# Meta tokens transposed first, one half tile normalised on ACT, and gate multiplications tied to adds in two blocks only: a decoder layer with PEER experts

## The chip, the cores and the metric

The kernel is one program on one core of a Trainium2 chip. The core has a matrix engine (PE, with its weight loads shown apart as PEld), a vector engine (DVE), an engine for activations and copies (ACT), a general engine (POOL) and a queue engine that only issues transfers (SP). Each runs its own list of instructions strictly in the listed order, and semaphores tie the lists together. The metric is the device time of one execution in microseconds (us), given as the median over runs.

## The reference

One post-norm layer over 256 tokens of width 2048, with 16 learned meta tokens put in front. All is float32.

```
h    = layer_norm(concat(meta, x))                     # 272 x 2048
proj = h @ w_in                                        # 2048 -> 8192
ya   = pool mixer (windows 2/4/8/16) -> pool_w -> pool_scale -> pool_proj
yb   = gated short convolution (width 3)              -> conv_proj
h    = layer_norm(ALPHA * h + (gate0*ya + gate1*yb) @ w_out)
# PEER: 8 heads, top 16 of 128 x 128 = 16384 single-neuron experts
q    = h @ w_q ; scores against keys_1, keys_2 ; top 16 of the sums
gate = softmax(top scores)
act  = gelu(h . expert_u[idx]) ; y = sum(gate * act * expert_v[idx])
out  = layer_norm(ALPHA * h + y)[:, 16:]
```

## The kernel before

**Precision.** Every matmul operand is split into a high part and a low part (`hi`, `lo`) of a fast float32 format, and three products are added. For weights, ACT casts the high part (`whi`, L95) and DVE or POOL subtracts it to get the low part (`wlo`, L74). Such a pair is 128 x 1024 and is called a half tile here; a 1 MB load (`raw`, L84, issued by SP, three buffers) holds two of them. `whi` and `wlo` have three buffers each, so DVE can be at most three half tiles ahead of PE.

**Start.** The meta tokens (`mt`, in a tile named `lng`) and the two token tiles `res[:, 0]` and `res[:, 1]` get their statistics on DVE. ACT normalises the meta tokens (L206), DVE both token tiles in halves of 1024 (L151). PE transposes them by pieces of 128 features into `acc` (L218, L219), each piece of tile 0 together with 16 meta columns, so that `ht` is 144 wide. ACT applies gain and shift (L222), DVE casts (L225) and subtracts (L74) into `h_hl`. The input projection (L102 to L104, L108, L109) needs all 272 columns of a piece.

**Experts.** All 16384 experts are computed densely for 224 tokens, as 128 groups of 128, with the routing gates spread into a table `G`; the last 32 tokens are done by gathers (`lone`, `urow`). An up tile (`up`, L627) multiplies by `expert_u`, giving `gl`; DVE adds its two halves (L113), ACT takes the gelu (L625). A block is four groups. For each block, `coef` (L644) multiplies `gl` by its gates (L648, DVE, four per block, called the gate multiplications), ACT casts the product to `c_hi` (L77) and DVE subtracts to `c_lo` (L74); `down` (L730) multiplies these by `expert_v` in two column halves, four half tiles each (L660), and DVE adds the results into `res` (L669).

**The order.** 44 up tiles run first (`LEAD`). Then each of 32 blocks does its two `down` halves, with two more up tiles ahead of each until all 128 are done; that is so through block 20, and blocks 21 to 31 have no up tiles. The table `G` lies in DRAM (`spill`); for a block, seven transfers of 64 KB bring it to one of two buffers (`fetch`, L742, issued by SP at L745, one block ahead in the program). A scheduler sets the order on each engine from the program's order, priorities and its own idea of when operands are there; `issue_after(x)` forces an instruction to stand behind `x`. In the kernel before every gate multiplication stands behind `last_on["dve"]`, the last weight subtraction or addition that the program had put on DVE by then.

Of the kernel before, what the change touches and what calls it, by code (L numbers as in the profile page):

```python
# [8 lines left out]
F32 = mybir.dt.float32  # L9
# [5 lines left out]
OP = mybir.AluOpType  # L15
# [3 lines left out]
P = 128  # L19
D = 2048  # L20
KD = D // P
T = 256
NT = T // P
META = 16
# [11 lines left out]
NB = 4  # L36
# [17 lines left out]
def block(ctx, tc, x, meta, w_in, small, pool_w, projs, w_out, wq, keys, eu, eur, ev,  # L54
          ln1_g, ln1_b, ln2_g, ln2_b, lin_g, lin_b, out):
    nc = tc.nc

    def pool(stack, name, bufs, side="left"):
        return stack.enter_context(tc.tile_pool(name=name, bufs=bufs, side=side, reuse_waits="tile"))
# [7 lines left out]
    def ps_mm():  # L67
        return mm.tile([P, 512], F32, name="mm")

    def ps_acc(t, c):  # L70
        return accp.tile([P, 512], F32, name=f"acc{t}{c}")

    def lo_part(lo, full, hi, eng=None):
        return (eng or nc.vector).tensor_tensor(lo, full, hi.bitcast(F32), op=OP.subtract)  # L74

    def split(hi, lo, full):
        nc.scalar.copy(hi, full)  # L77
        lo_part(lo, full, hi)
# [9 lines left out]
    last_on = {}  # L88
# [35 lines left out]
    ident = const.tile([P, P], F32, name="ident")  # L124
# [14 lines left out]
    def stats(st, src, c, n):  # L139
        nc.vector.bn_stats(out=st[:n, c, :], in_=src)  # L140

    def st_tile():
        return const.tile([P, 4, 6], F32, name="st", bufs=4)

    def mean_rstd(st, n):
        mv = const.tile([P, 2], F32, name="mv", bufs=4)
        nc.vector.bn_aggr(out=mv[:n], in_=st[:n])
        return mv, rstd_of(mv, n)

    def normalize(eng, dst, src, mv, r, n):  # L150
        eng.tensor_scalar(dst, src, mv[:n, 0:1], r[:n], op0=OP.subtract, op1=OP.mult)  # L151

    def shift_of(mv, r, n):
        shift = const.tile([P, 1], F32, name="shift", bufs=4)
        nc.vector.scalar_tensor_tensor(shift[:n], mv[:n, 0:1], -1.0, r[:n], op0=OP.mult, op1=OP.mult)
        return shift
# [13 lines left out]
    with ExitStack() as pa:  # L170
# [3 lines left out]
        a2 = pool(pa, "a2", 1)  # L174

        mt = lnp.tile([P, D], F32, name="lng")
# [9 lines left out]
        g_in = sm[:, 40:56]  # L186
        b_in = sm[:, 56:72]
# [6 lines left out]
        h_hl = hp.tile([P, KD, 2, TT], F32R, name="h_hl")  # L194
        nc.scalar.activation(neghalf, neghalf, AF.Identity)
        srcs = ((mt[:META], META), (res[:, 0], P), (res[:, 1], P))
        for i, (src, n) in enumerate(srcs):
            st = st_tile()
            for c in range(4):
                stats(st, src[:, c * 512:(c + 1) * 512], c, n)  # L200
            mv, r = mean_rstd(st, n)
            shift = shift_of(mv, r, n)
            for c in range(2):
                part = src[:, c * 1024:(c + 1) * 1024]
                if i == 0:
                    nc.scalar.activation(part, part, AF.Identity, bias=shift[:n], scale=r[:n])  # L206
                else:
                    normalize(nc.vector, part, part, mv, r, n)
        for t in range(NT):
            t0, n = (META + P, P) if t else (0, META + P)  # L210
            for k0 in range(0, KD, 2):
                ps = ps_acc(k0 // 2 % 2, k0 // 4 % 2).rearrange("p (k t) -> p k t", k=2)
                ht = a2.tile([P, 2, META + P], F32, name="ht", bufs=4)
                for i in range(2):
                    k = k0 + i
                    ks = slice(k * P, (k + 1) * P)
                    if t == 0:
                        nc.tensor.transpose(ps[:, i, 0:META], mt[:META, ks], ident[:META, :META])  # L218
                    nc.tensor.transpose(ps[:, i, n - P:n], res[:, t, ks], ident)  # L219
                for i in range(2):  # L220
                    k = k0 + i
                    nc.scalar.activation(ht[:, i, :n], ps[:, i, :n], AF.Identity,  # L222
                                         bias=b_in[:, k:k + 1], scale=g_in[:, k:k + 1])
                h_hi = h_hl[:, k0:k0 + 2, 0, t0:t0 + n]
                nc.vector.tensor_copy(h_hi, ht[:, :, :n])  # L225
                lo_part(h_hl[:, k0:k0 + 2, 1, t0:t0 + n], ht[:, :, :n], h_hi)
# [109 lines left out]
        for m in range(KD):  # L336
# [10 lines left out]
            for (hi, lo), y in zip(halves(parts, praw), (ya, yb)):  # L347
                ps = ps_mm()
# [207 lines left out]
    with ExitStack() as pb:  # L556
# [87 lines left out]
        def coef(e):  # L644
            gl = gels.pop(e)
            glv = gl.rearrange("p (g t) -> p g t", t=TG)
            with tc.issue_after(last_on["dve"]):
                nc.vector.tensor_tensor(glv, glv, Gs[e // NB][:, :, e % NB], op=OP.mult)  # L648
            c_hi = coefp.tile([P, TD], F32R, name="c_hi")
            c_lo = coefp.tile([P, TD], F32R, name="c_lo")  # L650
            split(c_hi, c_lo, gl)
            coefs[e] = (c_hi, c_lo)
# [129 lines left out]
        for e0 in range(0, NKEY, NB):  # L782
            es = range(e0, e0 + NB)
            if e0 and es[-1] < NKEY - 1:
                fetch(e0 // NB + 1)
            for e in es:
                coef(e)
            for dh in range(2):
                for _ in range(NB // 2):
                    if n_up < NKEY:  # L790
                        tick(up(n_up, (None, nc.gpsimd)))
                        n_up += 1
                if dh == 0 or es[-1] < NKEY - 1:
                    tick(down(es, dh))
# [106 lines left out]
```

## Time and profile before

| what | us |
|---|---|
| median of 3 runs | 2117.13 (2116.28 to 2117.24) |
| profiled execution, whole | 2117.67 |
| span of its trace | 2115.9 |
| PE busy in the span | 2054.7 (97%) |
| DVE busy | 1525.5 (72%) |
| ACT busy | 1001.8 (47%) |

The span is what the instructions of the trace cover; 1.8 us of the execution lie around it. PE is the engine to look at: it is busy 97% of the span, so a change of time is a change of the few per cent in which it waits, or of the clock that it is granted. A row of the timeline gives start, duration, engine, line, operation, what is written and read, and how often it repeats in sequence (x4); in brackets stands how long the engine had been idle and what released it.

### The profile page before, as it was taken

The numbers are of one execution on the slowest core, as the hardware profiler recorded it, in microseconds if no ns is written. First come the engines' busy times: TensorE is split into PE (matmuls) and PEld (weight loads), VectorE is DVE, ScalarE is ACT, GpSimd is POOL, SyncE is SP. The second block draws the span as 40 slices with busy tenths as digits, with TensorE's granted clock in tenths as the row PEclk, the third lists the DMA queues.
The fourth block names the chain that finished last, engine by engine and source line by source line (L and its number), as shares of the span: only waits on it lengthen the run. The fifth ranks groups of instructions, "written<-read, shape, count | busy, mean of one in ns | idle before, by whom it ended". The sixth has DMA issues, their size and how long they took to land.

```text
span 2115.9 us, 29922 instructions
## 1 busy us (share of the span) xinstructions
PE 2054.7 (97%) x11558; PEld 1770.5 (84%) x11558; DVE 1525.5 (72%) x2340; ACT 1001.8 (47%) x1424; POOL 600.8 (28%) x294
## 2 busy tenths in 40 slices
PE   7999999999999699999999999999999999999997
PEld 6999888888888689998888888888888888877765
DVE  7766666666779878836767776776677677788878
ACT  5444544444443356554444444444444445444442
POOL 0000000000065588883332333232334232300001
PEclk9999999999999799999999999999999999999998
DMA  5555555566553357787878777878787877877654
GB/s 202 219 180 182 195 181 191 187 224 233 191 183 125 107 202 273 264 284 274 292 266 291 272 269 268 291 269 289 262 283 268 293 260 275 278 271 270 224 169 158
DMA packets 114334, 498.09 MB, mean 235 GB/s; under 512 B 11200, under 2 KB 38336, under 8 KB 73344
## 3 DMA queue, kind: packets, MB, share of 16 engines
q1 hardware_dynamic: 103584, 413.61, 56.8%
q0 software_dynamic: 10608, 82.58, 10.0%
q8 instruction: 90, 1.47, 0.3%
q14 instruction: 52, 0.43, 0.1%
HBM read 478.32 MB, written 16.78 MB: 234 GB/s over the span
## 4 chain that ended last, share of the span: by engine, by line
PE 90%; DVE 7%; issue 1%; DMA 1%; POOL 1%; ACT 1%; SPq 0%; POOLq 0%; ACTq 0%
PE mm L108 28%; PE acc L660 27%; PE mm L109 14%; PE mm L660 5%; PE mm L103 2%; PE mm L102 2%; PE mm L104 2%; PE acc L116 2%; PE acc L117 2%; PE acc L118 2%; PE mm L595 1%; POOL wlo L74 1%; DMA raw<-in_eu 0%; DVE res L669 0%; PE acc L219 0%
## 5 line engine op out<-in xcount | busy, mean ns | idle before, releaser
L95 ACT CAST whi<-raw 128x1024 fp32r<-128x1024 f32 x738 | 772.2, 1048 | 801.5 <-PE mm L108 256.4
L74 DVE TENSOR_TENSOR wlo<-raw,whi 128x1024 fp32r<-128x1024 f32 x546 | 684.7, 1257 | 471.8 <-ACT whi L95 468.3
L108 PE MATMUL mm<-x_hl,whi 128*128 128x448 f32 x2048 | 656.1, 379 | 18.6 <-DVE gl L113 16.8
L74 POOL TENSOR_TENSOR wlo<-raw,whi 128x1024 fp32r<-128x1024 f32 x192 | 490.9, 2563 | 587.1 <-ACT whi L95 282.9
L109 PE MATMUL mm<-x_hl,wlo 128*128 128x224 f32 x2048 | 544.4, 266 | 6.3 <-POOL wlo L74 6.1
L108 PEld LDWEIGHTS mm<-x_hl,whi 128*128 128x128 f32 x2048 | 387.7, 189 | 50.4 <-issue 17.2
L109 PEld LDWEIGHTS mm<-x_hl,wlo 128*128 128x128 f32 x2048 | 394.9, 193 | 10.3 <-POOL wlo L74 8.0
L660 PE MATMUL acc<-whi,c_lo 128*128 128x512 f32 (+1 forms) x832 | 260.7, 395 | 5.0 <-DVE c_lo L74 5.0
L660 PE MATMUL acc<-whi,c_hi 128*128 128x512 f32 (+1 forms) x832 | 260.8, 395 | 4.3 <-ACT c_hi L77 4.3
L660 PE MATMUL acc<-wlo,c_hi 128*128 128x512 f32 (+1 forms) x832 | 260.7, 395 | 0.0
L108 PE MATMUL mm<-h_hl,whi 128*128 128x512 f32 x640 | 225.0, 395 | 0.0
L136 POOL TENSOR_TENSOR rstd<-rstd,neghalf 128x1 f32<-128x1 f32 (+1 forms) x7 | 5.8, 821 | 713.8 <-DVE rstd L135 697.5
L660 PEld LDWEIGHTS acc<-whi,c_lo 128*128 128x128 f32 (+1 forms) x832 | 146.4, 176 | 52.7 <-DVE c_lo L74 6.4
L660 PEld LDWEIGHTS acc<-wlo,c_hi 128*128 128x128 f32 (+1 forms) x832 | 146.2, 176 | 46.1 <-issue 0.2
L660 PEld LDWEIGHTS acc<-whi,c_hi 128*128 128x128 f32 (+1 forms) x832 | 143.0, 176 | 47.5 <-ACT c_hi L77 4.8
L109 PE MATMUL mm<-h_hl,wlo 128*128 128x256 f32 x640 | 180.5, 282 | 0.0
L669 DVE SCALAR_TENSOR_TENSOR res<-res,acc 128x512 f32<-128x512 f32 x208 | 131.6, 679 | 22.6 <-PE acc L660 20.7
L108 PEld LDWEIGHTS mm<-h_hl,whi 128*128 128x128 f32 x640 | 120.4, 188 | 26.9
L625 ACT ACTIVATE gl<-gl 128x224 f32<-128x224 f32 x128 | 49.7, 389 | 168.8 <-DVE gl L113 168.8
L109 PEld LDWEIGHTS mm<-h_hl,wlo 128*128 128x128 f32 x640 | 121.3, 189 | 0.0
L103 PE MATMUL mm<-h_hl,whi 128*128 128x258 f32 (+3 forms) x384 | 110.4, 288 | 0.0
L102 PE MATMUL mm<-h_hl,whi 128*128 128x258 f32 (+3 forms) x384 | 109.3, 285 | 0.0
(189 smaller groups left out, 2586.4 us busy)
## 6 DMA issues: line engine op xcount, KB each, us to landing
raw<-in_eu SPq DMA_DIRECT2D x128, 1024.0 KB, 6.0
raw<-in_ev SPq DMA_DIRECT2D x128, 1024.0 KB, 5.6
raw<-in_w_in SPq DMA_DIRECT2D x64, 1024.0 KB, 4.9
raw<-in_projs SPq DMA_DIRECT2D x16, 1024.0 KB, 4.9
raw<-in_w_out SPq DMA_DIRECT2D x16, 1024.0 KB, 5.0
raw<-in_wq SPq DMA_DIRECT2D x16, 1024.0 KB, 4.8
spill<-wide POOLq DMA_DIRECT2D x7, 2048.0 KB, 7.9
G<-spill SPq DMA_DIRECT2D x212, 64.0 KB, 5.1
```

The source lines that it names most:

```text
L74: return (eng or nc.vector).tensor_tensor(lo, full, hi.bitcast(F32), op=OP.subtract)
L95: last_on["act"] = nc.scalar.copy(hi, raw[:, s]).ins
L102: nc.tensor.matmul(ps, whi, xhi, start=first, stop=False)
L103: nc.tensor.matmul(ps, whi, xlo, start=False, stop=False)
L104: nc.tensor.matmul(ps, wlo, xhi, start=False, stop=last)
L108: nc.tensor.matmul(ps[:, :2 * n].rearrange("p (s t) -> p s t", s=2), whi, xhl, start=first, stop=False)
L109: nc.tensor.matmul(ps[:, :n], wlo, xhl[:, 0], start=False, stop=last)
L116: nc.tensor.matmul(ps, xhi, whi, start=first, stop=False)
L117: nc.tensor.matmul(ps, xhi, wlo, start=False, stop=False)
L625: nc.scalar.activation(gl, gl, AF.Gelu)
L660: nc.tensor.matmul(ps[c][:n_t], c_[:, ts], v_[:, c * 512:(c + 1) * 512], start=e == first and n == 0, stop=e == last and n == 2)
L669: nc.vector.scalar_tensor_tensor(r, r, 1.0 if (t, dh, c) in added else ALPHA, ps[c][:n_t], op0=OP.mult, op1=OP.add)
```

## The change

Three edits. The 16 meta transposes are taken out of the loop and done ahead into one tile `mm`; DVE applies gain and shift to all of them in two instructions, casts and subtracts them, and the token pieces shrink from 144 to 128 columns. The second half of `res[:, 0]` is normalised on ACT and no longer on DVE. The gate multiplications of blocks 0 and 1 stay behind the last DVE operation, those of blocks 2 to 31 are no longer tied to anything.

```diff
@@ -202,20 +202,27 @@
             shift = shift_of(mv, r, n)
             for c in range(2):
                 part = src[:, c * 1024:(c + 1) * 1024]
-                if i == 0:
+                if i == 0 or (i == 1 and c == 1):
                     nc.scalar.activation(part, part, AF.Identity, bias=shift[:n], scale=r[:n])
                 else:
                     normalize(nc.vector, part, part, mv, r, n)
+        pm = ps_mm()[:, :KD * META].rearrange("p (k t) -> p k t", k=KD)
+        for k in range(KD):
+            nc.tensor.transpose(pm[:, k], mt[:META, k * P:(k + 1) * P], ident[:META, :META])
+        hm = a2.tile([P, KD, META], F32, name="hm", bufs=1)
+        shape = [P, KD, META]
+        nc.vector.tensor_tensor(hm, pm, g_in[:, :, None].to_broadcast(shape), op=OP.mult)
+        nc.vector.tensor_tensor(hm, hm, b_in[:, :, None].to_broadcast(shape), op=OP.add)
+        nc.vector.tensor_copy(h_hl[:, :, 0, :META], hm)
+        lo_part(h_hl[:, :, 1, :META], hm, h_hl[:, :, 0, :META])
         for t in range(NT):
-            t0, n = (META + P, P) if t else (0, META + P)
+            t0, n = META + t * P, P
             for k0 in range(0, KD, 2):
                 ps = ps_acc(k0 // 2 % 2, k0 // 4 % 2).rearrange("p (k t) -> p k t", k=2)
-                ht = a2.tile([P, 2, META + P], F32, name="ht", bufs=4)
+                ht = a2.tile([P, 2, P], F32, name="ht", bufs=4)
                 for i in range(2):
                     k = k0 + i
                     ks = slice(k * P, (k + 1) * P)
-                    if t == 0:
-                        nc.tensor.transpose(ps[:, i, 0:META], mt[:META, ks], ident[:META, :META])
                     nc.tensor.transpose(ps[:, i, n - P:n], res[:, t, ks], ident)
@@ -644,7 +651,7 @@
         def coef(e):
             gl = gels.pop(e)
             glv = gl.rearrange("p (g t) -> p g t", t=TG)
-            with tc.issue_after(last_on["dve"]):
+            with tc.issue_after(last_on["dve"]) if e < 2 * NB else ExitStack():
                 nc.vector.tensor_tensor(glv, glv, Gs[e // NB][:, :, e % NB], op=OP.mult)
```

The lines behind the first edit shift by 7, so the gate multiplication is L648 before and L655 in the changed kernel, and the transfers of `G` are L745 and L752.

On DVE, at the start of block 0's first `down` half, the list before goes straight from the addition that ends an up tile (`gl_9605`) through the subtractions of the next half tiles (`wlo`).

```order
L74 TENSOR_TENSOR wlo_9665<-raw_9662,whi_9664 128x1024
L113 TENSOR_TENSOR gl_9605<-gl_9605,mm_9564 128x224
L74 TENSOR_TENSOR wlo_9681<-raw_9662,whi_9680 128x1024
L74 TENSOR_TENSOR wlo_9699<-raw_9696,whi_9698 128x1024
L113 TENSOR_TENSOR gl_9654<-gl_9654,mm_9611 128x224
L74 TENSOR_TENSOR wlo_9718<-raw_9696,whi_9717 128x1024
```

In the changed kernel the same place holds the gate multiplications of block 2 (reading `G_9917`) and of block 3 (`G_10293`); the numbers of the tiles are six higher here, so `wlo_9687` is the former `wlo_9681`.

```order
L74 TENSOR_TENSOR wlo_9671<-raw_9668,whi_9670 128x1024
L113 TENSOR_TENSOR gl_9611<-gl_9611,mm_9570 128x224
L655 TENSOR_TENSOR gl_6957<-gl_6957,G_9917 128x224
L655 TENSOR_TENSOR gl_7028<-gl_7028,G_9917 128x224
L655 TENSOR_TENSOR gl_7088<-gl_7088,G_9917 128x224
L655 TENSOR_TENSOR gl_7167<-gl_7167,G_9917 128x224
L74 TENSOR_TENSOR wlo_9687<-raw_9668,whi_9686 128x1024
L74 TENSOR_TENSOR wlo_9705<-raw_9702,whi_9704 128x1024
L113 TENSOR_TENSOR gl_9660<-gl_9660,mm_9617 128x224
L655 TENSOR_TENSOR gl_7245<-gl_7245,G_10293 128x224
L74 TENSOR_TENSOR wlo_9724<-raw_9702,whi_9723 128x1024
```

Blocks 2 to 12 follow in this manner between block 0's first half and block 1's second half in the list; from there each gate multiplication stands behind its own up tile. Block 1, which is still tied, comes after block 5. The sets of blocks 3, 4 and 5 thus pass through one of the two `G` buffers one after the other, since block 1's set holds the other.

On SP, in the same stretch, the list before has between two sets of seven `G` transfers six 1 MB loads (`raw`).

```order
L84 DMA raw<-in_eu 128x2048
L84 DMA raw<-in_ev 128x2x1024 x2
L84 DMA raw<-in_eu 128x2048 x2
L84 DMA raw<-in_ev 128x2x1024
L745 DMA G<-spill_6430 128x128
L745 DMA G<-spill_6431 128x128
L84 DMA raw<-in_ev 128x2x1024
```

In the changed kernel one load stands between two sets, or inside one.

```order
L752 DMA G<-spill_6442 128x128
L84 DMA raw<-in_eu 128x2048
L752 DMA G<-spill_6436 128x128
L752 DMA G<-spill_6437 128x128
L752 DMA G<-spill_6438 128x128
L752 DMA G<-spill_6439 128x128
L752 DMA G<-spill_6440 128x128
L752 DMA G<-spill_6441 128x128
L752 DMA G<-spill_6442 128x128
L84 DMA raw<-in_eu 128x2048
```

In the changed list twelve sets of seven (blocks 3 to 14) stand among 14 loads; in the list before there are eight loads to each set.

On DVE at the change from block 28 to 29, near the end, the list before has the gate multiplications and the `c_lo` of the new block in one piece, behind the additions of the old one.

```order
L721 SCALAR_TENSOR_TENSOR res<-res,urow 32x2048
L74 TENSOR_TENSOR wlo<-raw,whi 128x1024 x2
L669 SCALAR_TENSOR_TENSOR res<-res,mm 128x512 x2
L74 TENSOR_TENSOR wlo<-raw,whi 128x1024
L669 SCALAR_TENSOR_TENSOR res<-res,mm 96x512 x2
L648 TENSOR_TENSOR gl<-gl,G 128x224 x3
L74 TENSOR_TENSOR c_lo<-gl,c_hi 128x224 x3
L648 TENSOR_TENSOR gl<-gl,G 128x224
L74 TENSOR_TENSOR c_lo<-gl,c_hi 128x224
```

In the changed kernel no gate multiplication is left there, and the `c_lo` are spread, the first of them ahead of the additions.

```order
L728 SCALAR_TENSOR_TENSOR res<-res,urow 32x2048
L74 TENSOR_TENSOR wlo<-raw,whi 128x1024
L74 TENSOR_TENSOR c_lo<-gl,c_hi 128x224
L74 TENSOR_TENSOR wlo<-raw,whi 128x1024
L676 SCALAR_TENSOR_TENSOR res<-res,mm 128x512 x2
L676 SCALAR_TENSOR_TENSOR res<-res,mm 96x512
L74 TENSOR_TENSOR wlo<-raw,whi 128x1024
L676 SCALAR_TENSOR_TENSOR res<-res,mm 96x512
L74 TENSOR_TENSOR c_lo<-gl,c_hi 128x224 x2
```

PE's own list differs only in the first 110 instructions and by three pairs of matmuls near the end.

## Rows read from the trace of the kernel before

**Rows 1.** The page, busy time: engine, us, share, instructions.
```profile
PE 2054.7 (97%) x11558; PEld 1770.5 (84%) x11558; DVE 1525.5 (72%) x2340; ACT 1001.8 (47%) x1424; POOL 600.8 (28%) x294
```

**Rows 2.** Busy time by stretch: from:to, length, engines, PEclk, DMA, GB/s.
```profile
core 0: us, PE busy (x) PEld busy (x) DVE busy (x) ACT busy (x) POOL busy (x), PEclk, DMA share, GB/s
...
965.00:1050.00 85.00, 85.00 (x453) 72.44 (x452) 59.23 (x77) 41.38 (x58) 29.24 (x15) 1.00 0.81 292
...
1135.00:1843.00 708.00, 707.89 (x3747) 601.75 (x3746) 499.73 (x605) 336.97 (x471) 242.20 (x110) 1.00 0.78 277
...
1929.00:2014.00 85.00, 81.56 (x346) 61.22 (x345) 72.68 (x95) 38.12 (x48) 3.62 (x3) 0.98 0.72 243
2014.00:2094.90 80.90, 76.60 (x323) 57.90 (x323) 62.63 (x86) 33.67 (x40) 0.00 (x0) 0.96 0.53 176
```

**Rows 3.** PE's waits, 1843 to 2095: total us, times, longest.
```profile
PE acc L660 <- DVE c_lo L74: 5.0, 3, 1.8
PE acc L660 <- ACT c_hi L77: 4.3, 1, 4.3
```

**Rows 4.** PE alone by stretch: length, busy (instructions), granted clock, DMA, GB/s.
```profile
1868.50:1878.30 9.80, 9.58 (x42) 1.00 0.72 252
2005.30:2016.60 11.30, 11.13 (x42) 0.85 0.46 149
2031.80:2045.30 13.50, 13.45 (x49) 0.83 0.36 113
```

**Rows 5.** Timeline of DVE, block changes near the end.
```profile
1862.00 1.29 DVE L648 TENSOR_TENSOR gl<-gl,G 128x224 f32<-128x224 f32 x4
...
2031.00 0.98 DVE L648 TENSOR_TENSOR gl<-gl,G 128x224 f32<-128x224 f32 x3
```

**Rows 6.** Timeline of SP's queue, the seven transfers of block 2.
```profile
961.24 1.76 SPq L745 DMA_DIRECT2D G<-spill  x4
...
964.24 1.51 SPq L745 DMA_DIRECT2D G<-spill  x3
```

**Rows 7.** Tile G, issues between 964 and 967 (those three): time to landing.
```profile
DMA to landing us min/median/max: 5.1/7.4/9.7
```

**Rows 8.** Timeline of POOL's queue, gathers at the same time.
```profile
963.98 1.02 POOL L682 DMA_INDIRECT urow<-in_eur,lone_e  x1 [0.15 <-issue]
965.31 0.95 POOL L682 DMA_INDIRECT urow<-in_eur,lone_e  x1 [0.30 <-issue]
```

**Rows 9.** Timeline, same time: DVE, then PE's use of the second half tile.
```profile
965.16 0.37 DVE L113 TENSOR_TENSOR gl<-gl,mm 128x224 f32<-128x224 f32 x1
966.93 2.36 DVE L74 TENSOR_TENSOR wlo<-raw,whi 128x1024 fp32r<-128x1024 f32 x2 [1.40 <-ACT whi L95]
...
969.51 0.62 PE L660 MATMUL acc<-wlo,c_hi 128*128 128x512 f32 x2
```

**Rows 10.** Tile G, whole span: ns min/median/max, first and last start.
```profile
L745 SPq DMA_DIRECT2D G<-spill x210: 320/431/2012, 961.2 to 2036.0; - x105
L648 DVE TENSOR_TENSOR gl<-gl,G x128: 373/384/389, 959.0 to 2073.6; 128x224 f32<-128x224 f32 x128
...
DMA to landing us min/median/max: 1.8/5.2/10.4
```

**Rows 11.** The chain that ended last, two halves of block 0.
```profile
966.45 11.08 PE acc L660 x48
987.55 11.10 PE acc L660 x48
```

**Rows 12.** Timeline at the start: ACT, DVE, and PE's first projection matmul.
```profile
8.26 2.37 ACT L206 ACTIVATE lng<-lng,shift,rstd 16x1024 f32<-16x1024 f32 x2 [6.04 <-DVE shift L155]
...
11.16 1.53 DVE L151 TENSOR_SCALAR res<-res,mv,rstd 128x1024 f32<-128x1024 f32 x2
...
17.23 0.82 DVE L74 TENSOR_TENSOR h_hl<-ht,h_hl 128x288 fp32r<-128x288 f32 x2
...
23.72 0.56 PE L102 MATMUL mm<-h_hl,whi 128*128 128x258 f32 x1
...
24.27 0.76 DVE L74 TENSOR_TENSOR h_hl<-ht,h_hl 128x256 fp32r<-128x256 f32 x2
```

## Prediction

> **What bounds the kernel now.** I read the busy times first: PE works 97% of the span [rows 1]. So time can only come from PE's waits or from its clock. The busy time by stretch says where those are [rows 2]. Between 1135 and 1843 us PE works 707.89 of 708.00 us at the full granted clock, 1.00; there is nothing to win there. In the part without up tiles it loses 1843 to 2095 us, and the granted clock falls to 0.96. PE's waits in that part name the cause [rows 3]: three waits on `c_lo` (5.0 us) and one on `c_hi` (4.3 us), 9.3 us in all, each at a change of block. `c_hi` and `c_lo` come out of the gate multiplication. In the timeline of DVE these stand in one piece at the change (four in 1.29 us, [rows 5]), behind the additions of the old block; PE has nothing else to do then. After two of the waits PE also works at a lower clock [rows 4]: 42 matmuls take 11.13 us at a mean of 0.85, against 9.58 us for 42 at 1.00 (+1.55), and 49 take 13.45 us, where 49 x 0.228 = 11.18 would do (+2.27). A clock below 1.00 in these means is time spent at 1.2 GHz in place of 2.4. This is 3.8 us more, so 13.1 us hang on gates that come late.
>
> The second place to read is the start of block 0's first half, at 966 us, since the change moves twelve blocks' multiplications there. PE has no wait in that stretch: 85.00 of 85.00 us [rows 2]. But the DMA engines are busy 0.81 of it.
>
> **The tail: -13.1.** In the changed list no gate multiplication is left in blocks 21 to 31; they were done long before, `c_hi` depends on ACT alone, and the first `c_lo` stands ahead of the additions. What is late next is the subtraction of the next half tile on DVE, and DVE is ahead there in the stretches without a block change. So I take the whole: 9.3 + 3.8 = 13.1. The other end is 0: the waits stay because something else of the block change (the cast on ACT, the accumulators) binds.
>
> **The start: -0.3.** DVE loses one of two halves of a normalisation (1.53 / 2 = 0.77, [rows 12]) and the 144-wide pieces shrink: eight subtractions from 0.41 to 0.38 us, and I take as little for the casts, about -0.3 together. It gains four operations on 128 x 256, near the 0.38 us of the 128 x 224 multiplication [rows 10], 1.5 us. ACT gains one half tile, which lies near the 1.19 us of a 16 x 1024 one. PE's 16 meta transposes move ahead of the loop and are the same in number. If DVE's additions all lie in its idle time before the first transposes, the first projection at 23.72 us comes 1.1 us earlier; if none do, and the half tile on ACT is 0.4 us slower than on DVE, 0.8 us later. I take half of the additions as hidden: -1.1 + 0.8 = -0.3.
>
> **The rush, step 1: +7.8.** DVE runs its list in order, and in the changed list block 2's four gate multiplications stand behind the addition of `gl_9611` and ahead of the `wlo` of the second half tile. Before, DVE ends that addition at 965.53 and starts the two subtractions at 966.93 [rows 9]; PE takes the second one's result at 969.51. The gates must wait for the seven transfers of block 2. Four of these are issued from 961.24 on, three from 964.24 on [rows 6], the last about 965.3. These three land 5.1, 7.4 and 9.7 us after issue [rows 7], though the fastest of all 105 shown landings needs 1.8 [rows 10]; two indirect gathers go out on POOL just then [rows 8]. Nothing in the change moves them. So the last lands at 965.3 + 9.7 = 975.0 or little before, the gates take 1.3 [rows 5], the `wlo` 1.2 (half of 2.36, [rows 9]): 977.4 against 969.5, 7.8 us in which PE stands. Queued behind the waiting gate is every `wlo`, whose only reader is PE, and `wlo` has three buffers. With the median landing of 5.2 us it would be 965.3 + 5.2 + 2.5 - 969.5 = 3.5; with 1.8 it would be 0.1.
>
> By the row, a set of transfers beside gathers lands up to 9.7 us late. The Trainium skill (DMA: Bandwidth & Descriptors, Queues, rings and completion order) says that each DMA engine takes turns between the queue rows it has work for, a packet from each; with two rows at work a transfer would need about twice its 1.8 us, 3.6, and step 1 would cost 1.9 in place of 7.8. The trace gives the longer landings, so I go by it.
>
> **Step 2: +4.5.** Block 1 is still tied and holds one of the two `G` buffers until its own gates, which come behind block 5's. So blocks 3, 4 and 5 go through the other buffer one after the other: seven issues (7 x 0.431 = 3.0), the landing (5.2), four gates (1.3), 9.5 us each [rows 5, 10]. From 976.2 (the gates of block 2 done) three rounds less the last three gates (0.9), with a `wlo` (1.2): 976.2 + 28.5 - 0.9 + 1.2 = 1005.0. The `wlo` behind block 5's first gate is that of block 0's second half, 21.1 us later in PE's order [rows 11]: 969.5 + 21.1 + 7.8 = 998.4, and 2.1 more for the clock (below) makes 1000.5. So 4.5 us. It is 0 with the shortest landing, and with the longest of all (10.4, rows 10) three rounds of 14.7 make it about 20.
>
> **Step 3: +6.0.** Blocks 7, 8 and 9 each stand ahead of a further half tile. Two buffers are free by then, so a round comes every 9.5 / 2 = 4.75 us, while PE uses up a half tile in 12 matmuls, 12 x 0.228 = 2.74 us [rows 4]. Three times 2.0 is 6.0; the half tiles that stand without a round in front of them pay for block 10 and later. Bounds by the same landings: with 1.8 us 3 x 0.3 = 1, with 10.4 us 14.
>
> **The clock: +4.0.** Two of these waits are as long as the ones after which the trace shows the lower clock (1.8 and 4.3 us, [rows 3, 4]); by 1.55 and 2.27 for each I take 4.0. It is 0 if no wait is long, 6 if a third is.
>
> The Trainium skill (DMA: Bandwidth & Descriptors, Rules for kernel authors) advises to issue a transfer early, compute, and wait for it late. The change takes the gates of the tail out of the way by this, but in the rush the wait stands straight behind the issue. The rows price both, and the second is the greater.
>
> **The sum.** -0.3 - 13.1 + 7.8 + 4.5 + 6.0 + 4.0 = +8.9 us. The profiled execution takes 2117.67 us, 1.8 us more than its span; with it 2126.6. It lies 0.5 above the median of 2117.13, so the forecast for the median is 2126.0. With every bound at its low end (start -1.1, tail -13.1, step 1 0.1, step 3 1) it would be 2104; with every one at its high end (start +0.8, tail 0, 7.8 + 20 + 14 + 6), 2166.
>
> **Rivals.** *The rush is mostly absorbed* (no change). For: while PE stands, SP's 1 MB loads stop too, which leaves the DMA engines to `G`, and rounds get shorter than 9.5. Against: the first wait does not depend on it. Then 7.8 + 2.1 for the clock + 3.0 for all the rest is 12.9, against 13.4: -0.5, 2116.6.
>
> *Transfers land early* (faster). The place is the same, the price the landing time L. At L = 3 step 1 costs 965.3 + 3 + 2.5 - 969.5 = 1.3; step 2's rounds of 7.3 end at 969.6 + 21.9 + 0.3 = 991.8 against 969.5 + 21.1 + 1.3 = 991.9, so 0; step 3 costs 3 x (3.65 - 2.74) = 2.7; no clock is lost. 4.0 - 13.4 = -9.4, 2107.7. The same sum at L = 4.4 gives about 13, so from there down the kernel is faster. For: landings down to 1.8. Against: a median of 5.2, the DMA engines at 0.81, and the gathers beside the first set.
>
> *The tail's waits stay in part* (slower still). The `c_hi` of a block needs ACT, which shares the block change with the casts of weights, and the wait of 4.3 us was on ACT. With half of 13.1 left: 8.9 + 6.5 = 15.4, 2132.5. For: that wait. Against: it was inferred behind gates that came just before (2031.00, [rows 5]).
>
> *The untied gates do nothing*: excluded, since the order moves them for certain.
>
> **How the numbers follow.** The forecast, slower with both the gain and the rush, has a chance of 0.50; the tail kept in part 0.12; the rush absorbed 0.22; early landings 0.16. A difference of 0.2%, 4.2 us, is about what a measurement can tell from none here. So slower 0.62, the same 0.22, faster 0.16. The forecast's own range is 2121 to 2141. The range for all reaches down through the absorbed rush to 2112, which leaves out about half of the faster cases, and up to 2141, which leaves out landings beyond 7 us.
>
> **What would show it.** In the changed profile PE should have waits on DVE's `wlo` between 970 and 1045 us, 15 us or more in all, with DVE waiting for `G` before L655 at each; the first near 970 for about 8 us. After each long one the granted clock should dip. Behind block 21 no wait on `c_lo` or `c_hi` should be left, and PE should work at 1.00. The first projection should start at 23.4 us. I am wrong if block 2's transfers land by 970, if the rounds of blocks 3 to 5 take less than 7 us each, or if PE waits in the tail on another writer in place of `c_lo`.

## The result, and the profile after

The changed kernel takes 2133.5 us (median of 6 runs, 2131.07 to 2137.49) against 2116.05 us (6 runs) before: a ratio of 1.0083, with a 95% interval of 1.0071 to 1.0096. It is 17.4 us slower; the forecast was 2126.0 in a range of 2112 to 2141. The span of the profiled execution grew by 19.8 us, from 2115.9 to 2135.7.

The busy time by stretch of the changed kernel answers to [rows 2]; its columns are length, PE busy with instructions, granted clock, DMA share and GB/s.

```profile
965.00:1064.00 99.00, 75.92 (x349) 0.90 0.69 232
1843.00:2000.00 157.00, 156.90 (x705) 1.00 0.73 257
2000.00:2113.00 113.00, 113.00 (x492) 1.00 0.60 201
```

All the loss is in the first row: PE stands 23.1 of 99 us there and works at a mean clock of 0.90. The part without up tiles has become full, 269.9 of 270 us at 1.00, where the kernel before lost 9.3 us and clock. PE's waits between 965 and 1064 us give the writer:

```profile
PE acc L667 <- DVE wlo L74: 16.7, 5, 7.8
PE mm L109 <- DVE wlo L74: 6.2, 4, 2.6
PE mm L109 <- POOL wlo L74: 0.2, 1, 0.2
```

The timeline of PE shows them in brackets; here are the five longest of the ten. The first is the one that the prediction placed at 969.5 and sized 7.8:

```profile
977.84 1.22 PE L667 MATMUL acc<-wlo,c_hi 128*128 128x512 f32 x2 [7.85 <-DVE wlo L74]
...
997.98 0.52 PE L109 MATMUL mm<-x_hl,wlo 128*128 128x224 f32 x1 [2.57 <-DVE wlo L74]
...
1010.36 0.73 PE L667 MATMUL acc<-wlo,c_hi 128*128 128x512 f32 x2 [2.49 <-DVE wlo L74]
...
1034.57 0.73 PE L667 MATMUL acc<-wlo,c_hi 128*128 128x512 f32 x2 [3.41 <-DVE wlo L74]
...
1041.39 0.73 PE L667 MATMUL acc<-wlo,c_hi 128*128 128x512 f32 x2 [2.21 <-DVE wlo L74]
```

The other five are of 0.2 to 1.8 us, among them 0.75 at 985.87, 1.48 at 990.12 and 1.77 at 1053.43. Behind each of the five waits shown PE works at the lower clock, 1.2 GHz, for a stretch; the columns are those of the first view:

```profile
977.80:981.20 3.40, 3.36 (x8) 0.53 0.76 205
997.90:1001.60 3.70, 3.62 (x13) 0.54 0.71 232
1011.50:1015.30 3.80, 3.80 (x12) 0.55 0.85 313
1034.50:1038.50 4.00, 3.93 (x11) 0.64 0.93 336
1041.30:1045.30 4.00, 3.91 (x11) 0.64 0.78 270
```

PE's busy time in each row, times what its clock lacks to 1.00, gives 7.8 us for the five together; that is an estimate of what the lower clock costs. On DVE, the same stretch shows what it waits for. Each gate multiplication (L655) with a bracket stands ahead of a `wlo`:

```profile
965.45 0.38 DVE L113 TENSOR_TENSOR gl<-gl,mm 128x224 f32<-128x224 f32 x1
975.35 1.30 DVE L655 TENSOR_TENSOR gl<-gl,G 128x224 f32<-128x224 f32 x4 [9.52 <-issue]
976.56 2.35 DVE L74 TENSOR_TENSOR wlo<-raw,whi 128x1024 fp32r<-128x1024 f32 x2
...
984.29 0.39 DVE L655 TENSOR_TENSOR gl<-gl,G 128x224 f32<-128x224 f32 x1 [5.08 <-DMA G<-spill]
...
985.73 3.20 DVE L655 TENSOR_TENSOR gl<-gl,G 128x224 f32<-128x224 f32 x3
...
1008.78 0.39 DVE L655 TENSOR_TENSOR gl<-gl,G 128x224 f32<-128x224 f32 x1 [8.21 <-DMA G<-spill]
...
1010.22 0.99 DVE L655 TENSOR_TENSOR gl<-gl,G 128x224 f32<-128x224 f32 x3
...
1031.99 1.39 DVE L655 TENSOR_TENSOR gl<-gl,G 128x224 f32<-128x224 f32 x4 [1.50 <-DMA G<-spill]
...
1038.90 1.30 DVE L655 TENSOR_TENSOR gl<-gl,G 128x224 f32<-128x224 f32 x4 [4.09 <-DMA G<-spill]
```

Compare the first three with [rows 9]: the same two subtractions started at 966.93, now at 976.56. "issue" means that the profile shows no releaser for that wait; the next ones name the transfer. SP's queue shows why a set cannot go out earlier:

```profile
961.53 2.66 SPq L752 DMA_DIRECT2D G<-spill  x4
964.28 0.38 SPq L84 DMA_DIRECT2D raw<-in_eu  x1
964.71 13.71 SPq L752 DMA_DIRECT2D G<-spill  x7
```

The seven at 964.71 are block 2's last three and block 3's first four; the four stick until block 2's gates have freed the buffer, so the piece lasts 13.71 us, and the loads behind it on SP stand too.

To split the loss between waits and clock, I use the position of PE in the chain of waits. The fifth `down` half (48 matmuls) starts at 1050.93 before and at 1085.36 after.

```profile
1050.93 11.05 PE acc L660 x48
```

```profile
1085.36 11.05 PE acc L667 x48
```

That is 34.4 us later, and block 0 had begun only 0.3 us later (966.58 in the timeline of the changed kernel, 966.28 before). So the rush costs 34.1: 23.1 of waits, some 7.8 of lower clock by the estimate above, and a rest of 3.2. A part of the rest goes at each restart, where a pair of matmuls takes 0.73 us in place of 0.62 (1010.36 above, [rows 9]); for the other part no row is shown. From the 34.4 the end comes back to 19.8: the tail gives 14.6.

### The profile page after: what moved, and what is told of

The parts are those of the page before. It is cut to its first block, busy times and chain, and to the rows that moved or that the text cites. A ratio compares the mean times of both kernels' runs of the same rounds, so it can differ in the third digit from the quotient of the medians.

```text
span 2135.7 us, 29948 instructions
## 1 busy us (share of the span) xinstructions
PE 2059.0 (96%) x11558; PEld 1768.6 (83%) x11558; DVE 1549.0 (73%) x2343; ACT 1008.8 (47%) x1425; POOL 593.7 (28%) x294
## 4 chain that ended last, share of the span: by engine, by line
PE 87%; DVE 8%; DMA 2%; issue 2%; SPq 1%; POOL 1%; ACT 0%; DVEq 0%; POOLq 0%; ACTq 0%
PE mm L108 28%; PE acc L667 25%; PE mm L109 14%; PE mm L667 6%; PE mm L103 2%; PE mm L102 2%; PE mm L104 2%; PE acc L117 2%; PE acc L118 2%; PE acc L116 2%; PE mm L602 1%; DMA raw<-in_eu 1%; DMA G<-spill 1%; DVE wlo L74 1%; DVE gl L655 1%
## 5 line engine op out<-in xcount | busy, mean ns | idle before, releaser
L74 DVE TENSOR_TENSOR wlo<-raw,whi 128x1024 fp32r<-128x1024 f32 x546 | 675.7, 1242 | 393.8 <-ACT whi L95 389.8
L74 POOL TENSOR_TENSOR wlo<-raw,whi 128x1024 fp32r<-128x1024 f32 x192 | 484.5, 2529 | 617.9 <-ACT whi L95 318.8
L109 PE MATMUL mm<-x_hl,wlo 128*128 128x224 f32 x2048 | 544.2, 266 | 13.3 <-POOL wlo L74 7.1
L109 PEld LDWEIGHTS mm<-x_hl,wlo 128*128 128x128 f32 x2048 | 394.4, 193 | 18.3 <-POOL wlo L74 9.0
L109 PE MATMUL mm<-h_hl,wlo 128*128 128x256 f32 x640 | 180.2, 282 | 0.0
L109 PEld LDWEIGHTS mm<-h_hl,wlo 128*128 128x128 f32 x640 | 120.9, 189 | 0.0
```

The costliest lines, as they stand in the source:

```text
L109: nc.tensor.matmul(ps[:, :n], wlo, xhl[:, 0], start=False, stop=last)
```

## The experiments

Three theories were to be told apart: the loss is DVE's waits for the landings of `G` in the hoisted sets (A); part of it is the start's edits (B); or DVE is too full where 46 multiplications now stand in place of 8, between 965 and 1064 us (C). Each ratio is against runs of the kernel before on the same chip.

**The two halves of the change.** The first kernel has the start's edits alone:

```diff
-            with tc.issue_after(last_on["dve"]) if e < 2 * NB else ExitStack():
+            with tc.issue_after(last_on["dve"]):
```

> The start's edits alone (meta transposes first, half a tile on ACT); every gate multiplication tied as before. In the changed kernel's trace the first projection matmul starts at 22.89 us against 23.72 before, but by 672 us only 0.3 us of these 0.8 are left. Theory A (all of the slowdown is the waits for G in blocks 0 to 2): 0.3 to 0.8 us faster than before, near 2115.5, first projection at 22.9, no PE wait between 970 and 1060, the four waits near the end unchanged (9.3 us). Rival B (the split of h at the start also delays something later, such as the order of loads): slower than before by several us.

Measured: 2114.9 us against 2116.3, ratio 0.9994 (0.9985 to 1.0003). PE's waits behind 900 us are the old ones:

```profile
PE acc L667 <- DVE c_lo L74: 5.1, 3, 1.8
PE acc L667 <- ACT c_hi L77: 4.3, 1, 4.3
```

The start's edits are worth about 1 us or nothing; Theory B falls. The second kernel is the kernel before with the same line in its changed form:

> The gates alone: blocks 2 to 31 untied, the start as before. Theory A: PE loses the same 23 to 24 us of waits and about 10 us of clock between 965 and 1060 and wins 13 to 14 near the end, so 17 to 19 us slower than before, 2133 to 2135, about 0.5 above the changed kernel. Rival B (part of the loss is the start's): clearly below 2130.

Measured: 2138.1 us, ratio 1.0100 (1.0085 to 1.0116), 3 us beyond the range given. Its waits in the rush are the same kind, 23.9 us:

```profile
PE acc L660 <- DVE wlo L74: 21.8, 5, 7.7
PE mm L109 <- DVE wlo L74: 2.1, 2, 1.7
```

So the untied gates are the loss. That it is 4.6 us above the changed kernel, more than the start's edits alone gave, is not settled. Its granted clock from 965 to 1064 us is 0.86 against 0.90 in the changed kernel, so a part of it may be clock; why the waits fall otherwise there was not shown.

**The transfers taken away.** The changed kernel, with all gates reading the two first tables, which leaves the right gates out from block 2 on:

```diff
-                nc.vector.tensor_tensor(glv, glv, Gs[e // NB][:, :, e % NB], op=OP.mult)
+                nc.vector.tensor_tensor(glv, glv, Gs[e // NB % 2][:, :, e % NB], op=OP.mult)
...
-            if e0 and es[-1] < NKEY - 1:
-                fetch(e0 // NB + 1)
```

> The changed kernel without the transfers of G from block 2 on: the gate multiplications of all blocks read the two tables of blocks 0 and 1, which leaves the right gates of blocks 2 to 31 out. Everything else is the changed kernel's, but the scheduler may put the multiplications earlier still. Theory A (DVE waits for landings): the rush's 34 us go and the tail's 14 stay won, so before less 14 to 15: 2100 to 2103, and no PE wait between 970 and 1060 over 1 us. Rival C (DVE itself is too full there: 48 multiplications of 0.38 us, 18 us of work, are moved ahead into the blocks 0 to 2): waits of PE on wlo of 10 us or more stay, near 2115 to 2130.

Measured: 2109.3 us, ratio 0.9966 (0.9952 to 0.9979).

```profile
900.00:965.00 65.00, 57.61 (x396) 0.92 0.73 246
965.00:1064.00 99.00, 99.00 (x531) 1.00 0.76 276
...
1843.00:2090.00 247.00, 247.00 (x1074) 1.00 0.66 226
```

The rush is gone (99.00 of 99 us) and the tail's gain stays. It is still 6 us slower than expected, since a new loss appears at 900 to 965: without transfers to wait for, the scheduler puts 41 multiplications ahead of block 0, where the changed kernel has 4, and PE waits there (4.3 us on `whi`, 3.1 on a `wlo` of POOL). What ties these two waits to the multiplications is open.

This run can't part A from C for the blocks 0 to 2 either, since most of the multiplications left that stretch with the transfers. Between 965 and 1064 us the changed kernel has 46 of them and this one 19:

```profile
L655 DVE TENSOR_TENSOR gl<-gl,G x46: 375/384/2595, 975.3 to 1062.8; 128x224 f32<-128x224 f32 x46
```

```profile
L655 DVE TENSOR_TENSOR gl<-gl,G x19: 384/391/394, 966.4 to 1061.5; 128x224 f32<-128x224 f32 x19
```

What speaks for A is the changed kernel's own trace. Of its 23.1 us of waits, 13.3 (7.85, 0.75, 2.49 and 2.21) end with a `wlo` that stands right behind a gate for which DVE had stood idle over 4 us. The wait of 3.41 follows an idle time of only 1.50, with other work of DVE around it. The four waits on L109, 6.2 us, follow stretches in which DVE has no idle time for some 5 us or more, and one `wlo` in them takes 3.33 us in place of 1.2, beside a subtraction on POOL (993.76, 3.09 us):

```profile
994.60 3.33 DVE L74 TENSOR_TENSOR wlo<-raw,whi 128x1024 fp32r<-128x1024 f32 x1
```

What of these is DVE's added work and what is left over from the waits before, no run tells, so for some 6 to 8 us of the 23.1 C stays open.

**The gathers.** The gathers of the last 32 tokens begin some three blocks later:

```diff
-LONE_TICKS = 400
+LONE_TICKS = 340
...
-        lone_work, lone_rate = lone_rows(), (4 * NU + 4) / LONE_TICKS
+        lone_work, lone_rate, lone_credit = lone_rows(), (4 * NU + 4) / LONE_TICKS, -9.0
```

> The changed kernel with the gathers of the last 32 tokens begun some three blocks later (and then at a slightly higher rate), so that no gather goes out beside the transfers of block 2's gates; what is computed is the same. Theory A1 (the first wait of 7.85 us is long because two gathers share the DMA engines with those seven transfers): they land after 2 to 5 us, the first wait falls to 0 to 3.5 us, the half clock behind it goes too (3.4), and the later waits stay: 5 to 11 us faster than the changed kernel, 2123 to 2128. Rival A2 (the 1 MB loads alone make the landing long): the first wait stays at 7 us or more, 2132 to 2135.

Measured: 2122.6 us, ratio 1.0031 (1.0018 to 1.0044), so 11 us below the changed kernel. DVE's first wait for `G`, in its timeline:

```profile
966.32 1.30 DVE L655 TENSOR_TENSOR gl<-gl,G 128x224 f32<-128x224 f32 x4 [4.19 <-DMA G<-spill]
```

And PE's first wait:

```profile
968.81 0.73 PE L667 MATMUL acc<-wlo,c_hi 128*128 128x512 f32 x2 [2.47 <-DVE wlo L74]
```

DVE waits 4.19 in place of 9.52, PE 2.47 in place of 7.85, and the clock does not fall behind it. PE's waits on DVE's `wlo` in the rush come to 14.3 us, some 8.8 less. What was edited is the place and the rate of the gathers alone, so the long landing of block 2's set is theirs. Yet DVE's waits for `G` between 965 and 1064 us still sum to 28.2 us, in eleven pieces, against 28.4 in five in the changed kernel (18.9 put down to the transfers and 9.5 to "issue"). PE lost less although DVE waited as long: by these two traces it is the long single waits of DVE that cost PE, and not their sum.

**Other places for the ties.** One block tied, and 21:

```diff
-            with tc.issue_after(last_on["dve"]) if e < 2 * NB else ExitStack():
+            with tc.issue_after(last_on["dve"]) if e < NB else ExitStack():
```

> The changed kernel with the gate multiplications of block 0 alone tied, those of block 1 not. In its list blocks 2 and 3 go through one buffer straight behind each other ahead of a single half tile, and block 0's own gates, without which no down half can start, stand behind block 4's. Theory A (each hoisted set costs a fetch round of about 9.5 us in one buffer or 4.75 in two, less PE's 2.74 per half tile that stands between): two rounds ahead of one half tile alone are 14 to 19 us, with the later ones 30 to 45 us of waits and 8 to 15 of clock against 14 won in the tail, 2140 to 2165. Rival F (the loss is block 1's gates coming late, as they are still tied): the waits shrink, 2120 or less.

Measured: 2132.8 us, ratio 1.0074 (1.0057 to 1.0091): below the range given, and far above the rival's. DVE does wait longer for `G`:

```profile
DVE gl L655 <- DMA G<-spill: 42.6, 9, 7.9
```

But PE's waits on all engines between 900 and 1064 come to 24.9 us. The first two waits for `G` (7.68 and 7.92 us, ending at 935.85 and 952.44) fall among the last tiles of the lead, where POOL does the subtractions and DVE has none from 920 to 959 us. PE waits there too, 1.70 and 1.93 us, but on POOL's `wlo` and ACT's `whi`. The third (4.39 us, ending at 958.43) stands ahead of DVE's next `wlo`, and PE waits 5.00 us for it. A waiting DVE costs PE only what PE needs from DVE then. The second has `e < 21 * NB` in the same line:

> The changed kernel with blocks 0 to 20 tied and only blocks 21 to 31, which have no up tiles, untied. The scheduler then hoists these eleven blocks' gates to the blocks 19 and 20; in its list a set stands ahead of every one or two half tiles of DVE there, and both buffers rotate. Theory A (a round in two buffers takes 4.75 us, PE needs 2.74 per half tile and POOL does some of these): 0 to 2 us for each of eleven sets at about 1800 us, 0 to 15 us of waits with little clock, none near 970, none behind block 22: 2102 to 2116. Rival G (the loss belongs to the place: the gathers and block 1's buffer at block 0): no waits at all, the tail's gain whole, 2102 or less. Rival H (hoisting eleven blocks costs the same 34 us wherever it is): 2130 or more.

Measured: 2128.3 us, ratio 1.0056 (1.0039 to 1.0073), between A's range and H's. The rush moved with the tie:

```profile
965.00:1064.00 99.00, 99.00 (x524) 1.00 0.80 287
...
1700.00:1843.00 143.00, 126.12 (x623) 0.94 0.75 260
```

So G falls: it does not need block 0's place. A's price was too low: from 1762.12 to 1824.77 us seven sets of gates start, one every 10.4 us on average and not every 4.75. Three waits on DVE are long:

```profile
1771.71 0.39 DVE L655 TENSOR_TENSOR gl<-gl,G 128x224 f32<-128x224 f32 x1 [6.86 <-DMA G<-spill]
...
1799.79 1.30 DVE L655 TENSOR_TENSOR gl<-gl,G 128x224 f32<-128x224 f32 x4 [8.03 <-DMA G<-spill]
...
1824.77 1.30 DVE L655 TENSOR_TENSOR gl<-gl,G 128x224 f32<-128x224 f32 x4 [8.77 <-DMA G<-spill]
```

and ahead of each a gather goes out on POOL, at 1762.32, 1790.34 and 1813.41. A fourth, at 1830.28, is followed by a wait of only 1.43, so this is a sign of the gathers' part and no test of it.

**A version that beats both.** Each block's gates are tied to one mark earlier, so that they stand one block ahead and no more:

```diff
-            with tc.issue_after(last_on["dve"]) if e < 2 * NB else ExitStack():
+            with tc.issue_after(marks[-1] if NB < e < 31 * NB else last_on["dve"]):
...
+        marks = []
...
             for dh in range(2):
+                marks.append(last_on["dve"])
```

> The changed kernel, but each block's four gate multiplications are tied to the last DVE operation ahead of the previous block's second down half (blocks 2 to 30; blocks 0, 1 and 31 as before). In the list the set of G then stands two to eleven loads ahead of its gates, and the gates one block ahead of their use. Theory A: no rush, since one set is fetched per block; the tail's waits go but for one or two at blocks 29 to 31, so 8 to 14 us faster than before, 2102 to 2108. Rival D (it is any wait for G ahead of a wlo that costs, however the sets are spread): waits of some us at each block in the tail, where a block is 22 us, near before or slower.

Measured: 2103.0 us against 2116.3, ratio 0.9937 (0.9923 to 0.9951): 13.4 us faster than before.

```profile
965.00:1064.00 99.00, 99.00 (x521) 1.00 0.81 289
1843.00:2000.00 157.00, 157.00 (x683) 1.00 0.78 267
2000.00:2080.00 80.00, 78.58 (x342) 1.00 0.57 190
```

No rush, and the tail keeps one wait on `c_hi` of 1.42 us. DVE's waits between 960 and 2095 us, of which these are the two greatest, hold none for `G` any more:

```profile
DVE wlo L74 <- ACT whi L95: 242.4, 202, 3.7
DVE res L676 <- PE acc L667: 14.8, 17, 1.4
```

The landings are as slow as ever, in the view of tile `G`:

```profile
DMA to landing us min/median/max: 1.8/5.3/10.2
```

The distance between the issue and the gate has grown; the transfer has not got faster. Block 2's set is issued from 959.37 on and used at 1013.62, 54 us later, where the changed kernel has 14 (961.53 to 975.35). D falls.

## Why the prediction was right, and where it was off

- **The tail, -13.1.** Right: measured -14.6. All four waits went with their clock, and nothing late came in their place. The start-only kernel keeps them.
- **The start, -0.3.** The first projection came 0.8 us earlier (22.89 against 23.72), but block 0 began 0.3 later. The start-only kernel gives 1.4 us, with zero inside its interval. It was no term of weight.
- **Step 1, +7.8.** Right to a tenth: 7.85. It rested on the landing of 9.7 us in [rows 7]; the late gathers show that its cause was read rightly too. The tenth is luck: the price was one landing of one execution, and landings reach from 1.8 to 10.4 us in [rows 10]. (That row counts 210 transfers; the prediction's 105 is a misreading on which nothing rests.)
- **Steps 2 and 3, +10.5.** Measured 23.1 - 7.85 = 15.2: 7.3 up to and with the wait at 1010.36 (step 2, 4.5) and 7.9 behind it (step 3, 6.0). The step that failed is the round of "9.5 us each". From the end of block 2's gates (975.35 + 1.30) to the end of block 5's (1010.22 + 0.99) three rounds took 34.6 us, not 28.5. Two things were left out. Seven issues take more than 3.0 us: the sets of blocks 3 and 4 have a 1 MB load in their midst, and block 5's set takes 4.07 without one. In the middle round, of 10.2 us, DVE does not stand idle before the gates at all; its own other work set that length. Here are the last two sets on SP:

```profile
988.96 1.75 SPq L752 DMA_DIRECT2D G<-spill  x4
990.80 0.38 SPq L84 DMA_DIRECT2D raw<-in_ev  x1
991.23 1.48 SPq L752 DMA_DIRECT2D G<-spill  x3
...
999.16 4.07 SPq L752 DMA_DIRECT2D G<-spill  x7
```

And the gates do not run as a piece of 1.3 us: `wlo` stand between them, and the three at 985.73 took 3.20 us where the three at 1010.22 took 0.99, since one of them took 2.6, while POOL subtracted beside it:

```profile
985.87 2.51 POOL L74 TENSOR_TENSOR wlo<-raw,whi 128x1024 fp32r<-128x1024 f32 x1 [19.32 <-DVE wlo L74]
```

The Trainium skill (SBUF — State Buffer, SBUF: two separate sides) says that a DVE operation with two inputs from this memory and an operation of GpSimd (POOL here) that reads it share a pair of ports, which the one that starts first holds for its whole instruction. The 2.6 us against POOL's 2.51 agrees.

- **The clock, +4.0.** About 7.8 by the estimate above, near twice the term. The prediction counted two long waits; the trace has five of 2.2 us and more (7.85, 2.57, 2.49, 3.41, 2.21), each with a slow stretch behind it. In the kernel before only two of four waits had lost clock [rows 3, 4], and I carried over their number and not their share. The rest of 3.2 us, some of it at the restarts, had no term at all.
- **The sum.** +8.9 was forecast; the median moved by 17.4 and the profiled span by 19.8. Of the 10.9 us that lie between forecast and span, 4.7 are the rounds, 3.8 the clock, 3.2 the rest without a term, and 0.6 the start (0.3 late for 0.3 early); the tail gave 1.5 more. The direction and the mechanism were right; the range held although the rounds and the clock were both too low. The rival *early landings* needed landings under 4.4 us, with which block 2's gates would have started before 970 us (965.3 + 4.4 = 969.7); they started at 975.35. *Mostly absorbed* needed rounds shorter than 9.5, and they took 12.3, 10.2 and 12.1.

## What to carry to other kernels

Untying an instruction from its place does not only let it go where it was late; it lets a scheduler bring all its kind forward at once. Count then how many buffers its input has, and put one round of fetching (issue, landing, use) against each instruction of the same engine that stands behind it. A tie one stage earlier gave nearly the whole gain of the tail without the rush. Price a wait of the matrix engine with the lower clock and the restart that follow it: here they were half as much again.

## What the runs showed of the hardware

- The last of a set of seven 64 KB transfers landed up to 9.7 us after its issue where indirect gathers went out at the same time [rows 7, 8], and DVE's wait for the same set fell from 9.52 to 4.19 us when the gathers were moved. The three longest such waits of the kernel with 21 blocks tied each follow a gather.
- Behind waits of PE of 2.2 to 3.4 us TensorE's granted clock fell to 1.2 GHz for parts of the stretch from 965 to 1064 us, five times with that behind the first wait of 7.85; of the three waits of 1.6 to 1.8 us in the kernel before, one was followed by it.
